# Splitting posts, operand scaling and root computations into stages, one per step, in a one-core hybrid mLSTM / short-convolution block

## The chip, the cores and the metric

The kernel runs on one core of a Trainium2 chip. The metric is the device time of one execution in microseconds (us). Engines are written as in the profile: PE is TensorE, DVE is VectorE, ACT is ScalarE, POOL is GpSimd and SP is SyncE (which here only issues loads).

## What is computed

One residual block over 512 tokens of width 2048, in float32. Cut to what matters:

```
hn   = rmsnorm(x, norm_mix_g)
proj = hn @ w_in + b_in           # q, k, v, o, i, f, cb, cc, ch, gm, gc
hm   = mlstm(q, k, v, i, f)       # 4 heads, causal, per head an RMS norm at the end
y_m  = (hm * g * sigmoid(o)) @ w_branch_m
y_c  = (cb * causal_dwconv(cc * ch, conv_w)) @ w_branch_c
h    = x + (sigmoid(gm) * y_m + sigmoid(gc) * y_c) @ w_out
u    = causal_dwconv(rmsnorm(h, norm_ffn_g) @ w_up, ffn_conv_w, ffn_conv_b)
h    = h + (silu(gate) * val) @ w_down        # gate, val = halves of u
out  = rmsnorm(h, norm_out_g)
```

## The kernel before

**Steps and items.** All large products run through one hand-written loop of 492 steps, `for s in range(4, len(steps))` (L1203). An *item* is a pair of output blocks of 128 columns: 40 items of the x projection (numbers 0 to 39: q and k, v, o, cb, the conv pairs cc and ch as 16 to 23, then the gates gm and gc), 8 each for y_c, y_m and out, 43 for up, and three chunks of 8 for down; 16 short pieces end the program. A *step* is a quarter of an item (half of one for y_c and y_m) and holds 42 matmuls of 256 columns (48 in the last quarter of some), written by `cell_mm`. Float32 products are made of three passes over a high and a low half (`wh` with `xh`, `wh` with `xl`, `wl` with `xh`: L271 to L273), and a Strassen-like scheme makes 7 products of 8 out of sums of weight blocks.

**What the engines do in a step.** ACT copies the rounded high half of the next but one step's weights (`wh`, L225), DVE forms the low half (`wl`, L229) of the next step's, and sums of weight blocks (L210, L215). `wl` has three buffers and `wh` four. When an item ends, ACT evacuates one bank (L295) and DVE the others (L301 to L304, `evac_ops`) in the step that follows. Operand cells (activations) are prepared two steps ahead by `cell_task`: DVE's t3, e, t4 (L333, L338, L343), ACT's `hi` (L347), DVE's `lo` (L350). For the up items the cells come from h, scaled by the norm's gain: by ACT inside t3 (L331; L380 and L381 where the cell comes straight out of an item's buffer, `direct_cell`), followed at once by DVE's L333.

**Posts.** After its evacuation each item has a post: a list of pieces with costs. For q, k, v, gates and cb one piece multiplies by the row of 1/rms (`normed`, L642) and adds the bias or sigmoid on ACT, then stores. Conv items have four pieces (norm and bias; product and first tap; two taps; product with cb, store). Up items have four (norm and two biases; two taps and silu; two taps; product and store). Out items have two: residual, store of h and square on ACT (L764); then the sums of squares into mC (L769, L770), and after the last of them the norm's stages. Pieces are taken in order from one queue while a credit of DVE time lasts; an item about to lose its buffer forces what is left (`flush`), at the item end (L1275 on). Stores are issued by ACT in the step after.

**Side stages.** A queue `side` gives PE one extra piece per step, behind the step's matmuls, and its post runs in the next step, behind DVE's work for the weights. All of it shares one PSUM bank, SIDE (bank 7). The four heads of the mLSTM run there: load; `b_pe` / `b_post` four times (scores, exponentials on ACT, mask on POOL, product on DVE L577); `v_pe` / `v_post` twice (transposes); `c_pe` / `c_post` four times (values; then the head's norm, one root per block, L606 to L613); `t_pe` / `t_post` twice. Between two stages that fill SIDE lies an empty one (`gap`). The root (`rsqrt_cols`, L399) is a multiply-add on DVE (L403 or L405), a square root on ACT (L406), and a reciprocal with one Newton step on DVE (L407 to L411). `rows_stages` (L423) uses it for the norms over all tokens: root, four diagonal blocks on DVE (L428), a matmul into SIDE (L431), a copy into `rstd`.

The blocks c0 to c3 and t0 of head 0 are written at steps 52, 54, 56, 58 and 60, those of the later heads 24 steps later each. Every second of them (c2, t0) falls in a step that also evacuates an item.

Of the kernel before, what the change touches and what calls it, by code (L numbers as in the profile page):

```python
# [59 lines left out]
class Task:  # L60


    def __init__(self, load, sums, hi, lo, ready=None):
        self.load, self.sums, self.hi, self.lo, self.ready = load, sums, hi, lo, ready
        self.wh = self.wl = None
        self.raw, self.cost, self.plain, self.after_end = None, (0.8, 2.05), False, None
# [3 lines left out]
def tile_block(ctx: ExitStack, tc: tile.TileContext, xT, w1, w_v0, w_v1, w_v2, w_bm, w_bc, w_out, w_up, w_down,  # L70
# [236 lines left out]
    def cell_task(xs, c, d, scale=None, key=None, eight=False):  # L307

        k1, k2 = kpair(c) if isinstance(c, int) else c
        t = Task(None, None, None, None)  # L310

        def new_raw():
            t.raw = wp.tile([P, NW], F32, tag="raw", name=nm("xraw"), bufs=RAW)

        def load():
            new_raw()
            for dst, k in zip(t.two(), (k1, k2)):
                SP.dma_start(dst, d[k])

        def two_k():  # L320
            return (t.raw[:, :T], t.raw[:, T:2 * T]) if eight else (t.raw[:, 5 * SW:], t.raw[:, :2 * SW])

        def diff():
            x = slots(t.raw)
            V.tensor_sub(x[:, 4:6], x[:, 0:4:2], x[:, 1:4:2])

        def t3():
            x = slots(t.raw)
            if scale:
                for ap, k in zip(two_k(), (k1, k2)):  # L330
                    A.activation(ap, ap, AF.Copy, scale=scale(k))  # L331

            V.tensor_sub(x[:, 2:4], x[:, 1:6:4], two(x[:, 6]))  # L333
# [24 lines left out]
        t.ready = (lambda: all(k in stored for k in key)) if key else None  # L358
        return t

    def direct_cell(xs, c, it, d=None, scale=None, key=None, eight=False):

        t = cell_task(xs, c, d, None, key, eight)
        cell_t3, cell_load = t.sums[0], t.load
        k1, k2 = kpair(c)

        def load():
            if d is not None:
                cell_load()
            else:  # L370
                t.new_raw()

        def t3():
            assert it.done
            a, b = t.two()
            if d is not None:
                V.tensor_add(a, a, it.z[:, :T])
                V.scalar_tensor_tensor(b, it.z[:, T:], -1.0, b, op0=ALU.mult, op1=ALU.subtract)
            else:
                A.activation(a, it.z[:, :T], AF.Copy, scale=scale(k1))  # L380
                A.activation(b, it.z[:, T:], AF.Copy, scale=scale(k2))  # L381
            it.z_read = True
            cell_t3()

        it.z_read = False
        t.load, t.sums = load, [t3] + t.sums[1:]
        t.cost = (t.cost[0] + (1.35 if d is not None else 0), t.cost[1])
        t.after_end = it
        return t
# [9 lines left out]
    def rsqrt_cols(dst, src, scale, eps, n):  # L399

        v, y, t = sm("nv")[:, :n], sm("ny")[:, :n], sm("nt")[:, :n]
# [4 lines left out]
        A.activation(y, v, AF.Sqrt)  # L406
        V.reciprocal(y, y)  # L407
# [15 lines left out]
    def rows_stages(ps, dst, diag, nt=4):  # L423

        def cols_post():
            rsqrt_cols(rs1[:, :nt], ps[:, :nt], 1.0 / D, EPS, nt)
# [9 lines left out]
        return cols_post, rows_pe, rows_post  # L436
# [114 lines left out]
    def head_stages(h):  # L551
# [16 lines left out]
        def b_post(cs):  # L568
            def fn():
                w = T - cs * P  # L570
                p = S[:, So[cs]:So[cs] + w]
                for ct in range(cs, 4):
# [3 lines left out]
                                fill=0.0, base=0, channel_multiplier=-1)  # L576
                V.scalar_tensor_tensor(p, SIDE[:, :w], QK_SCALE, p, op0=ALU.mult, op1=ALU.mult)  # L577
# [25 lines left out]
        def c_post(ct):  # L603
            def fn():
# [7 lines left out]
                rsqrt_cols(ff[:, c], ssq[:, c], 1.0 / DV, den[:, c], 1)  # L612
# [34 lines left out]
    def qk_post(h):  # L647
        def post(it):
            a, b = halves(it)

            def fn():
                normed(it)
# [3 lines left out]
            return [(1.2, fn)]  # L656
        return post

    def v_post(h):
        def post(it):  # L660
            a, b = halves(it)

            def fn():
                normed(it)
# [3 lines left out]
            return [(1.2, fn)]  # L668
        return post

    def sig_post(d, c, j1, j2, key):
        def post(it):
            a, b = halves(it)

            def fn():
                normed(it)
# [3 lines left out]
            return [(1.2, fn)]  # L680
        return post

    def conv_post(j):
        def post(it):
            a, b = halves(it)

            def one():
                normed(it)
# [10 lines left out]
            def four():  # L699
                V.tensor_mul(a, a, mC)  # L700
                store(yc_d[j], a, ("yc", j))
            return [(1.2, one), (0.7, two_), (1.4, three), (0.7, four)]
# [16 lines left out]
    def cb_post(p):  # L719
        def post(it):  # L720
# [3 lines left out]
            def fn():  # L724
                normed(it)
# [3 lines left out]
            return [(1.2, fn)]  # L729
# [25 lines left out]
    acc = mC  # L755

    def out_post(p):
        def post(it):
            j1, j2 = kpair(p)

            def one():
                residual(it)
                store(pair_ap(h_d, j1, j2), sb_pair(it.z), ("h", p))
                A.activation(it.buf[:, :2 * T], it.z, AF.Square)  # L764
                it.done = True

            def two_():
# [5 lines left out]
                if p == 7:  # L773
                    cols, rows_pe, rows_post = rows_stages(SIDE, rstd, mC)
                    side.append((lambda: sum_tokens(SIDE, acc, 1, 4, True, True), cols))
                    side.append((noop, noop))
                    side.append((rows_pe, rows_post))
            return [(1.3, one), (1.4, two_)]
        return post

    def up_post(j):
        def post(it):
# [3 lines left out]

            def one():
                normed(it)
# [3 lines left out]
            def two_():  # L792
                V.scalar_tensor_tensor(y0[:, 1:], a[:, :T - 1], fwc(1, j), y0[:, 1:], op0=ALU.mult, op1=ALU.add)
                V.scalar_tensor_tensor(y0[:, 2:], a[:, :T - 2], fwc(0, j), y0[:, 2:], op0=ALU.mult, op1=ALU.add)
                A.activation(y0, y0, AF.Silu)
# [4 lines left out]

            def four():
# [256 lines left out]
    def flush(upto):  # L1058

        if posts and posts[0][2] <= upto:  # L1060
            while posts and posts[0][2] <= upto:
                posts.popleft()[1]()
            flush_late()
# [122 lines left out]
    cols, rows_pe, rows_post = rows_stages(SIDE, rstd, gb[5])  # L1186
    cols()
# [15 lines left out]
    for s in range(4, len(steps)):  # L1203
# [13 lines left out]
        for i in ended:  # L1217
            credit -= 2.3
            evs += evac_ops(i)
            for cost, fn in i.post(i):  # L1220
                posts.append((cost, fn, i.num))
# [14 lines left out]
        for t in cells_at.get(s + 2, []):  # L1236
            credit -= t.cost[0]
            load_to(t)
            sms += t.sums
# [49 lines left out]
        if s >= 4 + hold:  # L1289
            credit = min(credit, 2.5)  # L1290
            while posts and (credit > posts[0][0] / 2 or any(x[2] in urgent for x in posts) or not main):
                cost, fn, _ = posts.popleft()
                credit -= cost
                fn()
        if not main and it.n == 11:
            plain_rows = bank[3]
            cols, _, _ = rows_stages(LCOLS[0], None, mC, 2)
            cols()
# [16 lines left out]
    cols, _, _ = rows_stages(LCOLS[1], None, mC, 2)  # L1315
    cols()
# [62 lines left out]
```

## Time and profile before

| | us |
|---|---|
| median of 3 runs (2686.54 to 2688.54) | 2686.89 |
| the profiled execution's own time | 2686.18 |
| its span, first to last instruction | 2684.5 |
| PE busy | 2587.5 |
| DVE busy | 2112.7 |
| ACT busy | 1278.2 |
| granted PE clock, mean | 0.990 |

The span lies inside the execution's time; the rest is start and end. A line of the waits view reads: engine, tile and line that waited, what it waited for, us in total, times, longest. A line of the time line reads: start in us from the span's start, duration, engine, line, operation, output<-inputs, and in brackets the idle time of that engine just before and what ended it. A line of windows reads: the stretch, its length, then for PE, weight loads, DVE, ACT and POOL the busy time and count, then the granted PE clock (1.00 is full), the DMA engines' share and GB/s.

### The profile page before, as it was taken

To read this page: it belongs to the slowest core of one execution; us is meant where nothing else is said; L and a number is where in the kernel's file an instruction comes from. 1 tells how busy PE (TensorE), PEld (TensorE's weight loads), DVE (VectorE), ACT (ScalarE), POOL (GpSimd) and SP (SyncE) were. 2 spreads that over 40 slices of the span, in tenths; PEclk is the share of its full clock that TensorE was granted. 3 is DMA by queue.
4 is the path that set the end of the run, shared out by engine and by line. 5 is a ranking of instruction groups with operands and counts; after the bars stand their busy time and mean duration, and the time that the engine had idled before them with its cause. 6 is when DMAs were issued, how large, how long until landed. Compare 5 with 4: busy or idle time off the path is not lost.

```text
span 2684.5 us, 55468 instructions
## 1 busy us (share of the span) xinstructions
PE 2587.5 (96%) x21148; PEld 2564.8 (96%) x21148; DVE 2112.7 (79%) x3304; ACT 1278.2 (48%) x1735; POOL 801.6 (30%) x931
## 2 busy tenths in 40 slices
PE   7899999999999999999799999999999999999998
PEld 6899998999999999899799999999999989999997
DVE  5677777887777788977889988888888887676756
ACT  6444554445554443444545444444444554444433
POOL 3343333233333211121233333333333223232320
PEclk9899999999999999999999999999999999999999
DMA  7799989898989797797788888889888889798976
GB/s 193 177 230 235 246 228 229 215 243 223 253 228 233 205 297 221 212 252 207 204 223 219 223 222 225 221 222 228 218 222 227 206 216 226 188 226 207 238 173 200
DMA packets 464860, 594.64 MB, mean 222 GB/s; under 512 B 43040, under 2 KB 299040, under 8 KB 464592
## 3 DMA queue, kind: packets, MB, share of 16 engines
q1 hardware_dynamic: 303120, 420.84, 49.5%
q0 software_dynamic: 134240, 125.09, 31.6%
q10 hardware_dynamic: 27232, 45.17, 4.6%
q8 instruction: 165, 2.70, 0.4%
q14 instruction: 103, 0.84, 0.1%
HBM read 533.26 MB, written 57.67 MB: 220 GB/s over the span
## 4 chain that ended last, share of the span: by engine, by line
PE 52%; DVE 6%; DMA 4%; issue 2%; ACT 1%; POOL 0%; SPq 0%; DVEq 0%; POOLq 0%; ACTq 0%
PE bank L273 17%; PE bank L271 17%; PE bank L272 17%; DMA raw<-in_w_down_dram 2%; DVE wl L229 2%; DVE act L350 1%; DMA raw<-in_w_out_dram 1%; DMA raw<-in_w_up_dram 1%; DVE z L302 1%; DVE z L301 0%; PE bank L420 0%; PE bank L1095 0%; PE bank L1096 0%; DVE raw L210 0%; PE bank L1097 0%
## 5 line engine op out<-in xcount | busy, mean ns | idle before, releaser
L273 PE MATMUL bank<-act,wl 128*128 128x256 f32 x6760 | 1924.0, 285 | 39.3 <-DVE wl L229 35.9
L271 PE MATMUL bank<-act,wh 128*128 128x256 f32 x6760 | 1930.9, 286 | 14.7 <-DVE z L301 8.1
L272 PE MATMUL bank<-act,wh 128*128 128x256 f32 x6760 | 1919.7, 284 | 0.3 <-DVE act L350 0.3
L273 PEld LDWEIGHTS bank<-act,wl 128*128 128x128 f32 x6760 | 1304.2, 193 | 47.2 <-DVE wl L229 42.9
L271 PEld LDWEIGHTS bank<-act,wh 128*128 128x128 f32 x6760 | 1304.4, 193 | 19.3 <-DVE z L301 9.1
L272 PEld LDWEIGHTS bank<-act,wh 128*128 128x128 f32 x6760 | 1304.2, 193 | 3.6 <-issue 1.8
L225 ACT ACTIVATE wh<-raw 128x896 fp32r<-128x896 f32 x856 | 804.0, 951 | 1018.5 <-PE bank L272 682.0
L229 DVE TENSOR_TENSOR wl<-raw,wh 128x896 fp32r<-128x896 f32 x856 | 928.5, 1086 | 220.2 <-PE bank L273 149.6
L245 POOL DMA_DIRECT2D raw<-in_w_up_dram x344 | 299.1, 957 | 616.6 <-DMA raw<-in_w_up_dram 252.1
L245 POOL DMA_DIRECT2D raw<-in_w_dram x288 | 251.2, 950 | 551.2 <-DMA raw<-in_w_dram 274.3
L210 DVE TENSOR_TENSOR raw<-raw 128x256 f32<-128x256 f32 x428 | 179.2, 419 | 40.6 <-DMA raw<-in_w_down_dram 21.6
L245 POOL DMA_DIRECT2D raw<-in_w_down_dram x112 | 100.4, 1017 | 279.8 <-DMA raw<-in_w_down_dram 126.4
L215 DVE TENSOR_TENSOR raw<-raw 128x256 f32<-128x256 f32 x428 | 178.5, 417 | 0.2
L347 ACT ACTIVATE act<-xraw 128x1792 fp32r<-128x1792 f32 (+1 forms) x52 | 85.6, 1646 | 67.3 <-DVE xraw L343 56.6
L301 DVE TENSOR_TENSOR z<-bank,z 128x512 f32<-128x512 f32 x131 | 89.9, 686 | 28.4 <-ACT z L295 17.2
L183 ACT ACTIVATE wh<-raw 128x256 fp32r<-128x256 f32 x96 | 40.0, 416 | 130.1 <-PE bank L272 117.7
L350 DVE TENSOR_TENSOR act<-xraw,act 128x1792 fp32r<-128x1792 f32 (+1 forms) x52 | 101.7, 1956 | 0.0
L642 DVE TENSOR_TENSOR z<-z,rstd 128x1024 f32<-128x1024 f32 x83 | 101.0, 1218 | 0.0
L302 DVE TENSOR_TENSOR z<-bank,z 128x512 f32<-128x512 f32 x131 | 89.6, 684 | 1.8
L304 DVE TENSOR_TENSOR z<-bank,z 128x512 f32<-128x512 f32 x131 | 89.5, 683 | 0.0
L188 DVE TENSOR_TENSOR wl<-raw,wh 128x256 fp32r<-128x256 f32 x96 | 40.4, 421 | 57.9 <-PE bank L273 33.0
L245 POOL DMA_DIRECT2D raw<-in_w_out_dram x48 | 41.8, 972 | 129.6 <-DMA raw<-in_w_out_dram 64.0
(214 smaller groups left out, 1368.5 us busy)
## 6 DMA issues: line engine op xcount, KB each, us to landing
raw<-in_w_up_dram SPq DMA_DIRECT2D x172, 512.0 KB, 5.8
raw<-in_w_dram SPq DMA_DIRECT2D x144, 512.0 KB, 5.8
raw<-in_w_up_dram SPq DMA_DIRECT2D x344, 128.0 KB, 4.2
raw<-in_w_up_dram POOLq DMA_DIRECT2D x344, 128.0 KB, 5.1
raw<-in_w_down_dram SPq DMA_DIRECT2D x80, 512.0 KB, 5.2
raw<-in_w_dram SPq DMA_DIRECT2D x288, 128.0 KB, 4.1
raw<-in_w_dram POOLq DMA_DIRECT2D x288, 128.0 KB, 5.2
raw<-in_w_out_dram SPq DMA_DIRECT2D x32, 512.0 KB, 5.2
```

The source lines that it names most:

```text
L210: V.tensor_add(x[:, 6], x[:, 5], x[:, 0])
L215: V.tensor_add(x[:, 2], x[:, 6], x[:, 1])
L225: A.activation(seven(t.wh[r]), half(r), AF.Copy)
L229: V.tensor_sub(seven(t.wl[r]), half(r), seven(f(t.wh[r])))
L245: G.dma_start(at(i), a21, accum_op=ALU.add)
L271: PE.matmul(ps, h, xh, start=start, stop=False, skip_group_check=True)
L272: PE.matmul(ps, h, xl, start=False, stop=False, skip_group_check=True)
L273: PE.matmul(ps, l, xh, start=False, stop=stop, skip_group_check=True)
L301: return [lambda: V.tensor_add(z[:, 0:4:3], b0, two(z[:, 1])), lambda: V.tensor_add(z[:, 1:3], b1, two(z[:, 3])), lambda: V.tensor_add(z[: ...
L302: lambda: V.tensor_add(z[:, 1:3], b1, two(z[:, 3])),
L350: V.tensor_sub(t.act[:, NW:NW + m], t.raw[:, :m], f(t.act[:, :m]))
L642: V.tensor_mul(sb_pair(it.z), sb_pair(it.z), two(rstd))
```

## The change

The same instructions are issued with the same operands; their order and the step in which they stand change.

- *Posts.* The first piece of every post is now the norm on DVE alone; bias, sigmoid and store come as the next piece. Conv items: norm; bias; product and first tap; two taps, product with cb and store together. Up items: norm; biases; first two taps; silu and the other two taps; product and store. Out items: residual and store; square; sums. The queue holds items, not pieces: in a step at most one piece each of the first two items is taken. `flush` takes all that is left of an item at once.
- *Scaling.* ACT's scaling of a cell (`scaled`) is taken out of t3 and issued at the end of the step before, if the cell is loaded and the item is done; otherwise where it stood, before t3.
- *Roots.* `rsqrt_cols` becomes `rsqrt_a` (multiply-add and square root) and `rsqrt_b` (the rest). `c_post` keeps the first, and `c_post2` with `rsqrt_b` and ACT's last scaling (which reads SIDE) takes the place of the gap; `b_post2` with DVE's product (which reads SIDE) does so behind `b_post`. The norm before the up items gets one stage more, and an up item's norm asserts that it was issued.

The core of the diff:

```diff
@@ cell_task
+        def scaled():
+            for ap, k in zip(two_k(), (k1, k2)):
+                A.activation(ap, ap, AF.Copy, scale=scale(k))
         def t3():
             x = slots(t.raw)
-            if scale:
-                for ap, k in zip(two_k(), (k1, k2)):
-                    A.activation(ap, ap, AF.Copy, scale=scale(k))
...
+        t.pre = scaled if scale else None
@@ rsqrt
-    def rsqrt_cols(dst, src, scale, eps, n):
+    def rsqrt_a(src, scale, eps, n):
...
         A.activation(y, v, AF.Sqrt)
+
+    def rsqrt_b(dst, n):
+        v, y, t = sm("nv")[:, :n], sm("ny")[:, :n], sm("nt")[:, :n]
         V.reciprocal(y, y)
@@ heads
+        def b_post2(cs):
+            def fn():
+                w = T - cs * P
+                p = S[:, So[cs]:So[cs] + w]
                 V.scalar_tensor_tensor(p, SIDE[:, :w], QK_SCALE, p, op0=ALU.mult, op1=ALU.mult)
...
-                rsqrt_cols(ff[:, c], ssq[:, c], 1.0 / DV, den[:, c], 1)
+                rsqrt_a(ssq[:, c], 1.0 / DV, den[:, c], 1)
+            return fn
+
+        def c_post2(ct):
+            def fn():
+                c = slice(ct, ct + 1)
+                hn = z2[:, ct * DV:(ct + 1) * DV]
+                rsqrt_b(ff[:, c], 1)
                 A.activation(hn, SIDE[:, :DV], AF.Copy, scale=ff[:, c])
...
-            out += [(b_pe(cs), b_post(cs)), gap]
+            out += [(b_pe(cs), b_post(cs)), (noop, b_post2(cs))]
...
-            out += [(c_pe(ct), c_post(ct)), gap]
+            out += [(c_pe(ct), c_post(ct)), (noop, c_post2(ct))]
@@ posts (q and k; v, gates and cb alike)
             def fn():
-                normed(it)
                 A.activation(a, a, AF.Identity, bias=bias(C_Q + h))
...
-            return [(1.2, fn)]
+            return [(1.2, lambda: normed(it)), (0, fn)]
@@ conv_post
-            return [(1.2, one), (0.7, two_), (1.4, three), (0.7, four)]
+            return [(1.2, lambda: normed(it)), (0, one), (0.7, two_), (2.1, three)]
@@ out_post
             def one():
                 residual(it)
                 store(pair_ap(h_d, j1, j2), sb_pair(it.z), ("h", p))
+                it.done = True
+            def square():
                 A.activation(it.buf[:, :2 * T], it.z, AF.Square)
-                it.done = True
...
-                    side.append((lambda: sum_tokens(SIDE, acc, 1, 4, True, True), cols))
+                    side.append((lambda: sum_tokens(SIDE, acc, 1, 4, True, True), cols_a))
+                    side.append((noop, cols_b))
                     side.append((noop, noop))
-                    side.append((rows_pe, rows_post))
-            return [(1.3, one), (1.4, two_)]
+                    side.append((rows_pe, rows_post_up))
+            return [(1.3, one), (0, square), (1.4, two_)]
@@ up_post
-            return [(1.2, one), (1.4, two_), (1.4, three), (0.7, four)]
+            return [(1.2, norm), (0, one), (1.4, two_), (1.4, lambda: (silu(), three())), (0.7, four)]
@@ main loop
-            while posts and (credit > posts[0][0] / 2 or any(x[2] in urgent for x in posts) or not main):
-                cost, fn, _ = posts.popleft()
+            rush = not main or any(x[0] in urgent for x in posts)
+            for x in list(posts)[:2]:
+                cost, fn = x[1][0]
+                if not rush and cost and credit <= cost / 2:
+                    break
+                x[1].popleft()
                 credit -= cost
                 fn()
+                if not x[1]:
+                    posts.remove(x)
+        for t in cells_at.get(s + 3, []):
+            if t.pre and t.raw is not None and (not t.after_end or t.after_end.done):
+                t.pre()
+                t.pre = None
```

How the instructions move, on DVE. First, steps 55 and 56, in head 0 (den, nv, ny, nt and ff belong to the head's root; raw and wl to the weights; z and bank to the evacuation of an item). Before:

```order
L609 TENSOR_TENSOR den<-den,ecol 128x1
L610 TENSOR_TENSOR den<-den 128x1
L611 TENSOR_SCALAR den<-den 128x1
L405 SCALAR_TENSOR_TENSOR nv<-ssq,den 128x1
L407 RECIPROCAL ny<-ny 128x1
L408 TENSOR_TENSOR nt<-ny 128x1
L409 TENSOR_TENSOR nt<-nt,nv 128x1
L410 TENSOR_SCALAR nt<-nt 128x1
L411 TENSOR_TENSOR ff<-ny,nt 128x1
L210 TENSOR_TENSOR raw_3731<-raw_3731 128x256
```

After, the same place up to the second part of the root:

```order
L413 SCALAR_TENSOR_TENSOR nv<-ssq,den 128x1
L210 TENSOR_TENSOR raw_3731<-raw_3731 128x256
L301 TENSOR_TENSOR z_93<-bank_84,z_93 128x2x256
L215 TENSOR_TENSOR raw_3731<-raw_3731 128x256
L302 TENSOR_TENSOR z_93<-bank_85,z_93 128x512
L303 TENSOR_TENSOR z_93<-bank_85,z_93 128x256
L229 TENSOR_TENSOR wl_4008<-raw_3670,wh_3939 128x896
L304 TENSOR_TENSOR z_93<-bank_86,z_93 128x512
L229 TENSOR_TENSOR wl_4011<-raw_3670,wh_3993 128x896
L419 RECIPROCAL ny<-ny 128x1
L420 TENSOR_TENSOR nt<-ny 128x1
L421 TENSOR_TENSOR nt<-nt,nv 128x1
```

Reciprocal and Newton step moved from ahead of the next step's weights and evacuation to behind them.

Second, the change from out to up items, from the residual of the last but one out item (buffer mA) on; mC holds the sums of squares. Before:

```order
L752 TENSOR_TENSOR z_92<-mA,z_92 128x512
L753 TENSOR_TENSOR z_92<-mA,z_92 128x512
L769 TENSOR_TENSOR mC<-mC,mA 128x512
L770 TENSOR_TENSOR mC<-mC,mA 128x512
L210 TENSOR_TENSOR raw_14813<-raw_14813 128x256
```

After, where the residual is followed at once by the next step's L210 and the sums stand two steps further on:

```order
L351 TENSOR_TENSOR act_14956<-xraw_14742,act_14956 128x1792
L339 SCALAR_TENSOR_TENSOR xraw_14819<-xraw_14819 128x256
L344 SCALAR_TENSOR_TENSOR xraw_14819<-xraw_14819 128x256
L793 TENSOR_TENSOR mC<-mC,mA 128x512
L794 TENSOR_TENSOR mC<-mC,mA 128x512
L210 TENSOR_TENSOR raw_14963<-raw_14963 128x256
```

The sums moved from right behind the residual to two steps later, behind the cell work (act, xraw).

More of the change, by code (lines that the diff above doesn't have):

```diff
@@ L65, in __init__ @@
         self.wh = self.wl = None
-        self.raw, self.cost, self.plain, self.after_end = None, (0.8, 2.05), False, None
+        self.raw, self.cost, self.plain, self.after_end, self.pre = None, (0.8, 2.05), False, None, None
 @with_exitstack
@@ L375, in t3, with scaled @@
             a, b = t.two()
[L376 to L381, printed above, removed]
+            V.tensor_add(a, a, it.z[:, :T])
+            V.scalar_tensor_tensor(b, it.z[:, T:], -1.0, b, op0=ALU.mult, op1=ALU.subtract)
             it.z_read = True
             cell_t3()
-        it.z_read = False
-        t.load, t.sums = load, [t3] + t.sums[1:]
+        def scaled():
+            assert it.done
+            for ap, z, k in zip(t.two(), (it.z[:, :T], it.z[:, T:]), (k1, k2)):
+                A.activation(ap, z, AF.Copy, scale=scale(k))
+            it.z_read = True
+        it.z_read = False
+        t.load = load
+        if d is not None:
+            t.sums = [t3] + t.sums[1:]
+        else:
+            t.pre = scaled
         t.cost = (t.cost[0] + (1.35 if d is not None else 0), t.cost[1])
@@ L423, in rows_stages, with cols_a, cols_b @@
     def rows_stages(ps, dst, diag, nt=4):
-        def cols_post():
-            rsqrt_cols(rs1[:, :nt], ps[:, :nt], 1.0 / D, EPS, nt)
+        def cols_a():
+            rsqrt_a(ps[:, :nt], 1.0 / D, EPS, nt)
+        def cols_b():
+            rsqrt_b(rs1[:, :nt], nt)
             for t in range(nt):
@@ L773, in two_, with rows_post_up @@
                 if p == 7:
-                    cols, rows_pe, rows_post = rows_stages(SIDE, rstd, mC)
-                    side.append((lambda: sum_tokens(SIDE, acc, 1, 4, True, True), cols))
+                    cols_a, cols_b, rows_pe, rows_post = rows_stages(SIDE, rstd, mC)
+                    def rows_post_up():
+                        rows_post()
+                        normal["up"] = True
+                    side.append((lambda: sum_tokens(SIDE, acc, 1, 4, True, True), cols_a))
+                    side.append((noop, cols_b))
                     side.append((noop, noop))
-                    side.append((rows_pe, rows_post))
-            return [(1.3, one), (1.4, two_)]
+                    side.append((rows_pe, rows_post_up))
+            return [(1.3, one), (0, square), (1.4, two_)]
         return post
@@ L785, in post, with norm @@
             y0, y1 = buf[:, :T], buf[:, T:2 * T]
+            def norm():
+                assert normal["up"]
+                normed(it)
             def one():
-                normed(it)
                 A.activation(y0, a, AF.Identity, scale=fwc(2, j), bias=fwc(3, j))
@@ L799, in three, with silu @@
                 V.scalar_tensor_tensor(y1[:, 2:], b[:, :T - 2], fw_neg(0, j), y1[:, 2:], op0=ALU.mult, op1=ALU.add)
+            def silu():
+                A.activation(y0, y0, AF.Silu)
             def four():
@@ L1058, in flush @@
     def flush(upto):
-        if posts and posts[0][2] <= upto:
-            while posts and posts[0][2] <= upto:
-                posts.popleft()[1]()
+        if posts and posts[0][0] <= upto:
+            while posts and posts[0][0] <= upto:
+                for _, fn in posts.popleft()[1]:
+                    fn()
             flush_late()
@@ L1185, in tile_block @@
     A.activation(gb[4], GATE, AF.Copy, scale=mrow)
-    cols, rows_pe, rows_post = rows_stages(SIDE, rstd, gb[5])
-    cols()
+    cols_a, cols_b, rows_pe, rows_post = rows_stages(SIDE, rstd, gb[5])
+    cols_a()
+    cols_b()
     def rows_post2():
@@ L1219, in tile_block @@
             evs += evac_ops(i)
-            for cost, fn in i.post(i):
-                posts.append((cost, fn, i.num))
+            posts.append((i.num, deque(i.post(i))))
         ended = []
@@ L1314, in tile_block @@
         last_scale(0, finals.popleft(), row0)
-    cols, _, _ = rows_stages(LCOLS[1], None, mC, 2)
-    cols()
+    cols_a, cols_b, _, _ = rows_stages(LCOLS[1], None, mC, 2)
+    cols_a()
+    cols_b()
     PE.matmul(SIDE[:, :H2], ones, mC[:, :H2], start=True, stop=True)
```

26 lines of the change are left out of this document (12 added, 14 removed).

## The prediction

> **What bounds the kernel now.** I read the page's first part, then the waits of PE, then the windows and time lines of the places where PE waits.
>
> ```profile
> span 2684.5 us, 55468 instructions
> PE 2587.5 (96%) x21148; PEld 2564.8 (96%) x21148; DVE 2112.7 (79%) x3304; ACT 1278.2 (48%) x1735; POOL 801.6 (30%) x931
> ```
>
> PE is busy 96% of the span; no other engine comes near. So only PE's waits can change the time. The waits view, PE alone:
>
> ```profile
> PE bank L273 <- DVE wl L229: 35.9, 29, 3.7
> PE bank L271 <- DVE z L301: 8.1, 5, 3.2
> PE bank L584 <- ACT mB L593: 3.4, 2, 1.7
> PE bank L431 <- DVE mC L428: 3.3, 1, 3.3
> PE bank L621 <- DVE mB L627: 2.3, 4, 1.8
> ```
>
> PE waits for DVE's low halves of the weights (wl), for evacuations (z), and for stages on the shared SIDE bank. It is late only where DVE falls behind. Three places hold what the change touches: steps 223 to 229, where the out items hand over to the up items; some early up items; and the four mLSTM heads.
>
> The matmuls' own time, step 55 to 56 (head 0):
>
> ```profile
> 360.04 0.28 PE L273 MATMUL bank<-act,wl 128*128 128x256 f32 x1
> 360.16 0.28 PE L271 MATMUL bank<-act,wh 128*128 128x256 f32 x1
> 365.20 1.47 PE L600 MATMUL bank<-mB,mA 128*128 128x258 f32 x6
> ```
>
> Matmuls start 0.12 us apart but show 0.28, so a stall costs its idle time plus 0.16. Step 56 has 42 of them, from 360.16 to 365.20, and then c_pe, the head's matmul into SIDE. In the kernel before it starts at once.
>
> **Gain 1: steps 223 to 229.** DVE's and PE's waits between 1270 and 1335, then the rows of the second RMS norm's chain:
>
> ```profile
> DVE xraw L333 <- ACT xraw L381: 3.9, 3, 1.3
> DVE mC L769 <- ACT mB L764: 1.6, 1, 1.6
> DVE mC L769 <- ACT mA L764: 1.2, 1, 1.2
> ...
> 1318.80 0.15 DVE L403 TENSOR_SCALAR nv<-bank 128x4 f32<-128x4 f32 x1
> 1321.06 0.42 DVE L210 TENSOR_TENSOR raw<-raw 128x256 f32<-128x256 f32 x1
> ```
>
> DVE is the limit here: PE waits for its L301 and L229. The square gets a step of its own, so the sums L769 no longer wait (1.6 + 1.2 = 2.8). ACT scales the direct cells at the end of the step before, so L333 doesn't wait (3.9). The chain from L403 to L210 (2.26) moves one and two steps on, where DVE has caught up. Sum 9.0 us of DVE, and PE follows DVE: -9.0. What is late next: still L301 and L229, about 2 us a step until DVE has caught up, so nothing beyond this is won. Bounds: -4, if ACT (hi, then square, then scaling) is itself late and half of 9.0 returns; -10 with the chain's own PE wait (3.3) not fully counted.
>
> **Gain 2: up items**, PE's waits between 1385 and 1480:
>
> ```profile
> PE bank L273 <- DVE wl L229: 3.4, 4, 1.3
> ...
> DVE mB L793 <- ACT mB L789: 35.9, 19, 2.5
> DVE mA L793 <- ACT mA L789: 33.7, 19, 1.9
> ```
>
> (The last two are of the whole span.) The taps L793 wait 1.8 us each for the bias of the same step; a step apart they won't. Four PE stalls go: 3.4 + 4 x 0.16 = -4.0. The other 34 waits of DVE are covered by its slack already: nothing. Bounds -2 and -4.4.
>
> **Gain 3: heads.** PE's waits between 430 and 620:
>
> ```profile
> PE bank L273 <- DVE wl L229: 3.9, 3, 1.7
> PE bank L584 <- ACT mB L593: 3.4, 2, 1.7
> PE bank L621 <- DVE mB L627: 1.8, 1, 1.8
> ```
>
> They stem from conv posts bunched with head stages; spread over steps they go: 9.1, and 0.5 of L621 in the other heads, with 9 x 0.16: -11.0. Bounds -7 and -11.
>
> **Cost 1: the split root.** c_post2 runs in the very step at whose end PE overwrites SIDE (c_pe of the next block, or t_pe), and its last instruction reads SIDE. In the order before a whole step lay between. So PE waits where the end of c_post2 is later than the step's last matmul. Rows of head 0, DVE and ACT, and one table load of head 2:
>
> ```profile
> 357.91 1.09 DVE L229 TENSOR_TENSOR wl<-raw,wh 128x896 fp32r<-128x896 f32 x1 [1.97 <-PE bank L273]
> 358.92 0.15 DVE L609 TENSOR_TENSOR den<-den,ecol 128x1 f32<-128x1 f32 x1
> 359.56 0.16 DVE L405 SCALAR_TENSOR_TENSOR nv<-ssq,den 128x1 f32<-128x1 f32 x1
> 359.99 0.16 DVE L407 RECIPROCAL ny<-ny 128x1 f32<-128x1 f32 x1 [0.27 <-ACT ny L406]
> 361.79 0.69 DVE L301 TENSOR_TENSOR z<-bank,z 128x512 f32<-128x512 f32 x1 [0.53 <-ACT z L295]
> 366.39 1.22 DVE L642 TENSOR_TENSOR z<-z,rstd 128x1024 f32<-128x1024 f32 x1
> ...
> 358.89 0.20 ACT L608 ACTIVATION_READ_ACCUMULATOR z<-bank 128x1 f32 x1
> 359.75 0.20 ACT L406 ACTIVATE ny<-nv 128x1 f32<-128x1 f32 x1 [0.66 <-DVE nv L405]
> 361.01 0.47 ACT L613 ACTIVATE z<-bank,ff 128x256 f32<-128x256 f32 x1 [1.06 <-DVE ff L411]
> 361.39 0.38 ACT L295 ACTIVATE z<-bank 128x256 f32<-128x256 f32 x1
> ...
> 642.26 1.28 ACT L406 ACT_TABLE_LOAD   x1
> ```
>
> From L407 to the end of L613 is 359.99 to 361.48: 1.49 us. Each head waits four times.
> - Plain steps (c1, c3): wl is done at 358.92, 1.24 ahead of the matmuls' end (360.16), since wl has three buffers and must wait for PE. 1.49 - 1.24 and some 0.1 for signals: 0.4 each, 8 times, 3.2.
> - Steps that also evacuate an item (c2, t0), head 0: L405 ends 359.72, the root 359.95, L295 360.33, L301 starts 360.36; the evacuation and both wl take 361.79 to 366.39, 4.60: 364.96; plus 1.49: 366.45, against 365.20: 1.3 each, 2.6.
> - The same in heads 2 and 3: sigmoid posts lie between, so a table load (1.28) stands between L608's end (359.09) and the root, and once an ACT store (0.37): L301 at 361.0 to 361.4, and 1.9 to 2.3, say 2.1, four times: 8.4.
> - Head 1: the conv taps and the product now run as one stage in the step ahead of the evacuation:
>
> ```profile
> L697 DVE SCALAR_TENSOR_TENSOR z<-z,pneg 128x510 f32<-128x510 f32 x8 | 6.0, 750 | 0.3
> L696 DVE SCALAR_TENSOR_TENSOR z<-z,pneg 128x511 f32<-128x511 f32 x8 | 6.0, 744 | 0.0
> L700 DVE TENSOR_TENSOR z<-z,mC 128x512 f32<-128x512 f32 x8 | 5.5, 693 | 0.3
> ```
>
> Together 2.19: after 359.72 they put L210 (0.34) at 361.91, the evacuation's end at 366.85, L613's at 368.34, against 365.20: 3.2 each, two times, 6.4. By the same addition b_post2, moved a step on, makes v_pe or b_pe late three times in heads 1 and 2 (0.8, 0.8, 0.4): 2.0.
>
> Sum 3.2 + 2.6 + 8.4 + 6.4 + 2.0 = +22.6. No row of before shows c_pe waiting so; the nearest is L621 <- L627, a stage of the same step (2.3 in four waits). Bounds: 16 waits at the plain 0.4 give 6.4; 28 if stores and table loads all come late. I take the sum, since each term is an addition of rows. Behind the waiting PE stands all of the next step.
>
> **Cost 2: the clock.** Three stretches with stalls:
>
> ```profile
> 459.90:469.52 9.62, 6.19 (x51) 5.78 (x50) 9.24 (x14) 4.75 (x8) 3.11 (x5) 1.00 0.78 187
> 1294.45:1305.07 10.62, 8.58 (x50) 8.12 (x51) 8.91 (x15) 5.67 (x6) 1.75 (x2) 0.68 0.57 153
> 2227.50:2237.60 10.10, 7.06 (x44) 6.65 (x44) 9.44 (x14) 2.42 (x4) 2.60 (x3) 0.83 0.73 161
> ...
> 2233.18 0.38 PE L271 MATMUL bank<-act,wh 128*128 128x256 f32 x1 [2.45 <-ACT z L295]
> ```
>
> The first holds two stalls of 1.7 and keeps full clock; the third holds one of 2.45 and has 0.83; the second, behind one of 3.2, has 0.68. So between 1.7 and 2.45 us of waiting PE's clock begins to fall; 0.83 of 10.10 is 1.7 us lost. Head 1's two waits of 3.2 would cost 1.7 each: +3.4. Bounds 0 and +10 (the four waits of 2.1 too). The Trainium skill ("TensorE: Matmul & The Clock Gate", Part 1: The HAM clock gate) says that the clock halves after at least one idle window of about 3.4 us, which is free-running: by it 3.2 us would cost nothing and the sum would be 3.4 lower. The trace's 2.45 speaks against that.
>
> In steps 223 to 229 the same fall costs nothing of its own, as DVE is the limit there.
>
> **Cost 3: the change to the down items.** At the end of steps 403 and 407 the posts of the items before must be done at once (flush), and the evacuation L295 queues on ACT behind their store:
>
> ```profile
> 2232.37 0.33 ACTq L147 DMA_DIRECT2D a_d<-mB  x1
> ```
>
> PE waits for that L295 until 2233.18 (above). With one stage per step, norm (1.22, row 366.39) and two taps that had run a step earlier now stand in front of that store as well: about 2.7 us more DVE work in that step, less 1.4 that it no longer carries over: 1.3 later. In 407 the same list meets a step that had slack: 1.3 again. +2.6; bounds 0 and +5.
>
> **Covered.** ACT gets three table loads more (3 x 1.28): ACT is busy 48%, and only the two on the root's way are counted (above). SP's load of sigmoid(o) into mB comes one step later, still a step ahead of its reader. Nothing else is added or removed: the same instructions in another order.
>
> **Sum**, on the profiled execution's own 2686.18 us (span 2684.5 and 1.7 around it): -9.0 - 4.0 - 11.0 + 22.6 + 3.4 + 2.6 = +4.6, 2690.8. That execution is 0.7 below the median of the runs, 2686.89, so against it 2691.5: 0.17% slower. What a measurement here can tell from no change is about 0.2%, 5.4 us.
>
> **Rivals.**
> - *The clock doesn't fall* (chance 0.15): both 3.2-us waits end before the clock reacts, and PE goes on at full rate. For it: the two stalls of 1.7 with clock 1.00; against: 2.45 with 0.83. Sum +1.2: 2688.1. The rule of the Trainium skill quoted above would have it so.
> - *Slower* (0.22): the waits of 2.1 us in heads 2 and 3 fall on the clock's side too. One mechanism: a wait over about 2 us in c2 or t0 halves the clock, 4 x 1.7 = +6.8: 2698.3. It decides from the point where L301 starts over 0.8 us into the step. For it: 2.1 is nearer to 2.45 than to 1.7; against: the two stalls of 1.7 in one stretch kept theirs.
> - *Faster* (0.13): the 16 waits are all near the plain 0.4, because without L613 ahead of L295 the evacuation starts early enough and DVE catches up. Then 6.4 + 2.0 and no clock loss: -9.0 - 4.0 - 11.0 + 8.4 + 2.6 = -13.0: 2673.9. Against it: 4.60 us of evacuation and wl follow L301 back to back in the rows, whatever comes before.
> - *Nothing is moved* (0.05): the freed waits were hidden by other waits that come next, and c_post2 is hidden too: 2686.9. Against it: PE's waits in the three places name just these instructions.
>
> **Chances.** My forecast, +4.6 and some 4 us to either side, has 0.45: two thirds of it (0.30) within 5.4 us, the rest (0.15) slower. With the clock rival (0.15) and nothing moved (0.05) within, that is same 0.50; slower 0.15 + 0.22 = 0.37; faster 0.13. The range takes in the slower rival and 4 us of its unknown costs, and downward the removal of gains at full with waits half as long: 2681 to 2702; what is left out is most of the faster rival and costs at their upper ends together.
>
> **What would show it.** In the changed kernel's profile: DVE no longer waits for ACT at the sums and at L334 (L333 before), nor at the up taps; PE reaches step 230 about 9 us sooner after step 223 begins; between 1385 and 1480 PE has no stall. In the heads PE's waits name ACT's scaling L641 (L613 before), 16 times, some 20 us, longest 3.2, and PEclk falls near steps 80 and 84. Wrong would be: c_pe waiting under 8 us in total (then it is faster), PE stalls left in steps 224 to 229 of the old size, or a new wait in a phase that I left out, yc to out.

## The result, and the profile after

The changed kernel took 2694.4 us (median of 14 runs, 2687.54 to 2698.05), the kernel before 2686.31 (14 runs beside it, 2680.35 to 2692.99): ratio 1.0031, 95% interval 1.0022 to 1.0041. It is slower, by 8 us. Runs of one kernel scatter by some 5 us to either side, so single terms below come from the traces, and the times carry the sums.

Top of the page and PE's waits in the kernel after, to be laid beside those of before. A line number of after is up to some 35 higher: L580 is b_pe, L621 c_pe, L649 t_pe, L641 the last scaling of the head (L613 before).

```profile
span 2692.6 us, 55546 instructions
PE 2589.0 (96%) x21148; PEld 2565.4 (95%) x21148; DVE 2111.6 (78%) x3304; ACT 1284.0 (48%) x1738; POOL 805.4 (30%) x931
```

```profile
PE bank L273 <- DVE wl L229: 27.0, 19, 3.7
PE bank L271 <- ACT z L295: 11.0, 4, 5.6
PE bank L621 <- ACT z L641: 8.0, 8, 2.9
PE bank L649 <- ACT z L641: 7.4, 4, 2.9
PE bank L580 <- DMA mB<-qk_d: 5.3, 2, 3.3
PE bank L271 <- DVE z L301: 4.5, 3, 3.3
```

The busy times are nearly those of before. The waits for DVE's weights and evacuations fell (35.9 to 27.0, 8.1 to 4.5), the wait for the norm's matmul is gone, and so are those for L593 and L627. New are 15.4 us for the head's last scaling; the wait for the load of q and k rose from 0.9 to 5.3, and that for the first evacuation, L295, from 6.7 to 11.0. The windows between the same steps say where the time went; first the kernel before: steps 41 to 136 (heads), 223 to 230, 230 to 404, 404 to 409.

```profile
280.30:804.93 524.63, 514.13 (x4168) 506.37 (x4167) 397.26 (x698) 275.30 (x419) 170.21 (x210) 1.00 0.90 233
1277.05:1334.82 57.77, 43.64 (x312) 41.26 (x311) 48.12 (x75) 30.63 (x36) 13.96 (x16) 0.91 0.73 191
1334.82:2227.56 892.74, 882.94 (x7323) 880.51 (x7321) 787.92 (x1148) 435.12 (x532) 300.11 (x346) 1.00 0.88 223
2227.56:2258.53 30.97, 27.93 (x219) 27.52 (x218) 26.20 (x40) 12.78 (x20) 9.41 (x10) 0.94 0.75 170
```

And after, between the same steps:

```profile
280.82:825.68 544.86, 523.63 (x4169) 513.72 (x4167) 400.00 (x698) 279.53 (x422) 174.38 (x209) 0.98 0.88 224
1297.81:1346.28 48.47, 41.62 (x310) 40.25 (x309) 45.86 (x66) 29.05 (x34) 13.80 (x16) 0.93 0.82 214
1346.28:2232.51 886.23, 880.70 (x7324) 879.08 (x7323) 784.00 (x1155) 436.34 (x530) 298.89 (x345) 1.00 0.89 225
2232.51:2266.60 34.09, 27.81 (x218) 27.40 (x217) 26.08 (x40) 14.84 (x22) 11.28 (x12) 0.90 0.78 178
```

The heads lost 20.2 us, and the clock there is 0.98 instead of 1.00. The change from out to up won 9.3, the up items and what follows 6.5; the first down items lost 3.1. Sum: +7.5, of the span's 8.1.

Why the heads lost: step 80 (c2 of head 1) in the kernel after, DVE, then ACT, then PE. Its matmuls began at 497.52 and ended at 502.56.

```profile
496.93 0.16 DVE L413 SCALAR_TENSOR_TENSOR nv<-ssq,den 128x1 f32<-128x1 f32 x1
497.01 0.75 DVE L720 SCALAR_TENSOR_TENSOR z<-z,pneg 128x511 f32<-128x511 f32 x1
499.52 0.68 DVE L301 TENSOR_TENSOR z<-bank,z 128x512 f32<-128x512 f32 x1
504.11 0.16 DVE L419 RECIPROCAL ny<-ny 128x1 f32<-128x1 f32 x1
...
505.13 0.47 ACT L641 ACTIVATE z<-bank,ff 128x256 f32<-128x256 f32 x1 [3.49 <-DVE ff L423]
...
505.66 2.40 PE L621 MATMUL bank<-mB,mA 128*128 128x258 f32 x6 [2.94 <-ACT z L641]
```

Taps and product (497.01 to 499.18) stand ahead of the evacuation, the evacuation and the weights (4.59 from L301 on) ahead of the root's second part, and ACT's scaling is done 3.1 us after PE could have begun c_pe. This is the chain of the prediction.

And the clock, behind that wait (steps 80 and 81), behind the load at step 89, and behind a wait of 1.7 us (step 104):

```profile
497.50:507.40 9.90, 6.96 (x49) 6.45 (x48) 9.66 (x19) 3.32 (x5) 1.72 (x2) 0.94 0.71 182
507.40:513.70 6.30, 6.30 (x45) 6.18 (x44) 2.45 (x8) 1.58 (x5) 1.75 (x2) 0.82 0.70 148
555.90:565.20 9.30, 6.04 (x49) 5.83 (x48) 7.00 (x10) 3.47 (x4) 1.75 (x2) 0.95 0.96 257
565.20:572.90 7.70, 7.70 (x44) 7.70 (x44) 2.09 (x3) 2.64 (x3) 3.62 (x5) 0.62 0.82 222
643.40:651.50 8.10, 6.40 (x51) 6.06 (x49) 7.20 (x15) 3.79 (x7) 1.72 (x2) 1.00 0.89 248
```

The first pair lost 9.90 x 0.06 + 6.30 x 0.18 = 1.7 us of clock, the second 0.5 + 2.9 = 3.4, the last nothing. The load at step 65, for which PE waits 2.0 us, is followed by a fall too: half the clock for 3.45 us, 1.7 us lost.

```profile
420.90:424.35 3.45, 3.45 (x18) 3.45 (x18) 0.00 (x0) 0.00 (x0) 1.35 (x2) 0.51 0.67 251
```

### The profile page after: what moved, and what is told of

Read it like the earlier page. It is cut to its first block, busy times and chain, and to the rows that moved or that the text cites. A ratio compares the mean times of both kernels' runs of the same rounds, so it can differ in the third digit from the quotient of the medians.

```text
span 2692.6 us, 55546 instructions
## 1 busy us (share of the span) xinstructions
PE 2589.0 (96%) x21148; PEld 2565.4 (95%) x21148; DVE 2111.6 (78%) x3304; ACT 1284.0 (48%) x1738; POOL 805.4 (30%) x931
## 4 chain that ended last, share of the span: by engine, by line
PE 81%; DVE 8%; DMA 4%; issue 2%; ACT 1%; POOL 0%; SPq 0%; DVEq 0%; ACTq 0%; POOLq 0%
PE bank L273 26%; PE bank L271 26%; PE bank L272 26%; DVE wl L229 2%; DMA raw<-in_w_down_dram 2%; PE bank L621 1%; DVE act L351 1%; DMA mB<-qk_d 1%; DVE z L302 1%; PE bank L432 0%; DVE z L304 0%; PE bank L1131 0%; DVE z L301 0%; DMA raw<-in_w_up_dram 0%; PE bank L1132 0%
## 5 line engine op out<-in xcount | busy, mean ns | idle before, releaser
L225 ACT ACTIVATE wh<-raw 128x896 fp32r<-128x896 f32 x856 | 813.1, 953 | 1083.7 <-PE bank L272 726.3
L210 DVE TENSOR_TENSOR raw<-raw 128x256 f32<-128x256 f32 x428 | 180.0, 421 | 42.1 <-DMA raw<-in_w_down_dram 23.6
L301 DVE TENSOR_TENSOR z<-bank,z 128x512 f32<-128x512 f32 x131 | 89.8, 685 | 27.7 <-ACT z L295 17.6
```

The lines of the kernel that those rows point to most:

```text
L210: V.tensor_add(x[:, 6], x[:, 5], x[:, 0])
L225: A.activation(seven(t.wh[r]), half(r), AF.Copy)
L301: return [lambda: V.tensor_add(z[:, 0:4:3], b0, two(z[:, 1])), lambda: V.tensor_add(z[:, 1:3], b1, two(z[:, 3])), lambda: V.tensor_add(z[: ...
```

## The experiments

All of them compute the whole block. The ratios are to the kernel before, which ran beside each; the changed kernel's is 1.0031.

**c_whole: the head's root in one piece again**

```diff
-            out += [(c_pe(ct), c_post(ct)), (noop, c_post2(ct))]
+            out += [(c_pe(ct), lambda a=c_post(ct), b=c_post2(ct): (a(), b())), gap]
```

> The changed kernel with the head's root in one piece again: c_post does what c_post and c_post2 do, and an empty stage follows, as before the change; all other splits stay. Theory (PE waits because c_post2 reads SIDE in the step at whose end PE overwrites it): the 12 waits for L641 (15.4 us idle, some 17 with 0.16 each) and the clock that falls behind the two of 2.9 us (about 2.5) go, little comes back: about 19 us less than the changed kernel, 2675, ratio to the kernel before 0.996. Rival 1 (the root's DVE work costs the same wherever it stands, PE then waits for wl instead): ratio stays at 1.003. Rival 2 (the late loads of q and k into mB, 5.3 us of PE waits in the changed kernel, also come from c_post2, which issues a load one step later): 8 us more go, ratio 0.993.

Measured: 2676.56 us, ratio 0.9959 (0.9947 to 0.9971). PE's waits in its heads (300 to 830):

```profile
PE bank L580 <- DMA mB<-qk_d: 4.2, 2, 2.9
PE bank L649 <- DVE mB L655: 2.4, 4, 1.0
PE bank L273 <- DVE wl L229: 0.4, 1, 0.4
```

All waits for L641 are gone and wl takes their place with 0.4 only, so rival 1 falls. (The 2.4 us at L655 stood in the kernel before too, 2.3 at L627.) The loads of q and k are still waited for, so rival 2 falls too. One line of the change turns the gain of the rest into a loss.

**root_only: the kernel before with the split root alone**

```diff
-                rsqrt_cols(ff[:, c], ssq[:, c], 1.0 / DV, den[:, c], 1)
+                rsqrt_a(ssq[:, c], 1.0 / DV, den[:, c], 1)
+            return fn
+
+        def c_post2(ct):
...
-            out += [(c_pe(ct), c_post(ct)), gap]
+            out += [(c_pe(ct), c_post(ct)), (noop, c_post2(ct))]
```

> The kernel before with one part of the change alone: c_post split into c_post and c_post2. Theory: 16 waits at c1, c2, c3 and t0, 0.4 in plain steps and 1.3 to 3.2 where an item is evacuated, and some clock: +15 to +24 us, ratio 1.006 to 1.009. Rival (the wait is hidden where posts run as before the change, or the other splits cause it): within 3 us, ratio 1.000.

Measured: 2698.46 us, ratio 1.0042 (1.003 to 1.0054), so about +11 by the ratio. PE's waits in its heads; its lines L608, L636 and L628 are c_pe, t_pe and the scaling:

```profile
PE bank L608 <- ACT z L628: 6.8, 7, 1.8
PE bank L636 <- ACT z L628: 4.5, 4, 1.3
PE bank L592 <- ACT mB L601: 2.2, 2, 1.5
PE bank L273 <- DVE wl L229: 2.1, 1, 2.1
PE bank L573 <- DMA mB<-qk_d: 0.7, 2, 0.4
```

The split alone slows the kernel, and the rival falls; but less than expected. By the lengths of the sixteen steps that end with such a wait (from a step's first main matmul to the next step's) the split costs 16.0 us here, inside the expectation. But old stalls shrink beside it (steps 74, 85 and 98 by 2.2, 1.9 and 2.3), which the expectation left out. Where posts run as before, no taps stand ahead of the evacuation and no table load ahead of the root there, so c2 and t0 cost PE 1.3 to 1.5 in every head. The clock stays at 1.00 in these heads, behind the 2.1 us for wl (step 70) too:

```profile
441.10:454.30 13.20, 11.12 (x89) 10.53 (x87) 11.26 (x17) 6.48 (x10) 2.40 (x4) 1.00 0.82 186
```

The long waits of the changed kernel are the split root and the split posts together. The load is waited for 0.7 only, and step 89 is as short as in the kernel before (5.2 us): the late load at head 2 comes with the posts.

**c_copy: c_post2 doesn't read SIDE**

```diff
+                A.activation(hn, SIDE[:, :DV], AF.Copy)     # at the end of c_post
-                A.activation(hn, SIDE[:, :DV], AF.Copy, scale=ff[:, c])
+                A.activation(hn, hn, AF.Copy, scale=ff[:, c])
```

> The changed kernel, but c_post copies SIDE to z2 unscaled (one ACT instruction of about 0.47 us more per block), and c_post2 scales z2 in place, so c_post2 no longer reads SIDE. It computes the same. Theory (it is the read of SIDE that PE waits for): the waits of c1 to c3 go (0.4, 1.3 to 3.2 and 0.4 per head, 8.0 us idle by the profile of the changed kernel, some 9 with 0.16 each, and about 1 to 1.5 of clock), those of t0 stay (7.4 idle), since it reads what c_post2 writes: about 10 to 13 us less than the changed kernel, ratio 0.998 to 0.9995. Rival (PE waits because DVE is late with the root, whichever bank is read; wl would be late next): no gain, ratio 1.003.

Measured: 2679.31 us, ratio 0.9974 (0.9961 to 0.9988). PE's waits in the heads:

```profile
PE bank L650 <- ACT z L642: 7.0, 4, 2.6
PE bank L580 <- DMA mB<-qk_d: 4.4, 3, 2.9
```

All eight c_pe waits are gone and the four of t_pe stay, though DVE's root is just as late (in step 80 its second part begins 6.6 us into the step in both kernels). So at c_pe it is the read of the shared bank that held PE, as the theory says; t_pe waits for the scaled values themselves. The gain is about 15 us, 2 more than its upper end, of which the load at step 65 and the clock behind it are some 3 (a wait that scatters, see below).

**conv_early: a shorter conv piece ahead of the evacuation**

```diff
-            return [(1.2, lambda: normed(it)), (0, one), (0.7, two_), (2.1, three)]
+            return [(1.2, lambda: (normed(it), one())), (0.7, two_), (1.4, three), (0.7, four)]
```

> The changed kernel with the conv posts in another division: norm and bias in one step, product and first tap in the next, two taps in the third, and in the last step of the item only the product with cb (0.69 us on DVE) instead of taps and product (2.19). Theory (the waits of head 1 at c2 and t0 are long because 2.19 us stand ahead of the evacuation, and a wait of 2.9 us lets the clock fall where one of 1.7 does not): these two waits shrink by about 1.5 each, and two clock falls (about 1.2 each) go: 5 to 5.5 us less than the changed kernel, ratio 1.001. Rival 1 (the clock falls all the same): 3 us less, ratio 1.002. Rival 2 (the length of the conv piece does not matter): ratio 1.003.

Measured: 2684.27 us, ratio 0.9994 (0.9985 to 1.0002). Waits in the heads, and steps 80 and 81:

```profile
PE bank L621 <- ACT z L641: 6.0, 5, 1.7
PE bank L649 <- ACT z L641: 5.8, 4, 1.7
PE bank L580 <- DMA mB<-qk_d: 3.2, 1, 3.2
```

```profile
493.50:501.20 7.70, 6.34 (x49) 6.02 (x48) 7.53 (x17) 3.65 (x6) 1.72 (x2) 1.00 0.81 219
501.20:506.50 5.30, 5.30 (x45) 5.25 (x45) 3.12 (x8) 1.81 (x6) 1.75 (x2) 1.00 0.87 188
```

No wait for L641 is longer than 1.7, and the clock stays at 1.00 behind them: both as expected, so both rivals fall. (The profile is of an execution 5 us above the median.) The time fell by 10 instead of 5. In the two profiles the load at head 1, not waited for here (2.0 in the changed kernel), makes up 3.6 of the heads' 10.6. But up to that load both kernels run the same instructions in the same order, so that wait comes and goes between executions, and why the medians differ by 5 us more than expected stays open.

**no_pre: c_whole without the early scaling**

```diff
-            if t.pre and t.raw is not None and (not t.after_end or t.after_end.done):
+            if False:
```

> The changed kernel with the head's root in one piece (c_whole), and besides with ACT's scaling of the up items' cells back in the step of the subtraction that needs it. Theory (in steps 223 to 229 DVE is the limit and waits for this scaling): DVE's waits for ACT at L334 return, 3.9 us as in the kernel before, and PE gets to step 230 about 3 to 4 us later than in c_whole: 2680, ratio 0.9973. Rival (the gain in these steps comes from the sums and the root alone, the scaling is hidden since the square no longer stands ahead of it on ACT): no difference from c_whole, ratio 0.996.

Measured: 2681.72 us, ratio 0.9976 (0.9965 to 0.9987): about 4.5 more than c_whole, with intervals that just overlap. DVE's waits between 1255 and 1330:

```profile
DVE xraw L334 <- ACT xraw L325: 4.1, 4, 1.6
DVE xraw L334 <- ACT xraw L386: 3.9, 3, 1.3
```

The 3.9 are back to the digit, and so are the waits for L325, the scaling of cells that were loaded from memory (L331 in the kernel before: 5.1 between the same times). Steps 223 to 229, in c_whole and then here:

```profile
1278.87:1326.73 47.86, 41.34 (x311) 40.18 (x310) 45.37 (x66) 28.80 (x33) 13.12 (x16) 0.93 0.81 214
1278.22:1332.84 54.62, 44.16 (x310) 42.83 (x309) 48.71 (x73) 31.91 (x36) 14.81 (x17) 0.88 0.80 212
```

The scaling is worth 6.8 us in these steps, more than the 3 to 4 expected, and also where the square no longer stands ahead of it; the rival falls. (The other kernels that scale early take 47.1 to 48.7 here.)

**qk_first: the load of q and k ahead of the gates**

```diff
+            SP.dma_start(qk[:, :2 * T], qk_d[h])
             SP.dma_start(S[:, :T], gates_d[32 * h:32 * h + 1, :].to_broadcast([P, T]))
-            SP.dma_start(qk[:, :2 * T], qk_d[h])
```

> c_whole with the head's load of q and k into mB issued ahead of the broadcast load of the gates instead of behind it. Theory (PE waits at b3 of heads 1 and 2 because this load takes 10 us, in the queue behind 256 KB of the gates and beside the weights): the load lands 1 to 2 us sooner, the two waits of 4.2 us in total become 1 to 2, and the clock falls behind neither: 3 to 5 us less than c_whole, ratio 0.9945. Rival (the load waits for the store of the head before out of mB, not for the queue, or all queues share what the engines move): no difference, ratio 0.996.

Measured: 2672.32 us, ratio 0.9943 (0.993 to 0.9955), 4 less than c_whole, with overlapping intervals. One wait for the load is left, at head 2:

```profile
PE bank L580 <- DMA mB<-qk_d: 1.6, 1, 1.6
```

**tail: the last up posts without waiting for credit**

```diff
-            rush = not main or any(x[0] in urgent for x in posts)
+            rush = not main or any(x[0] in urgent for x in posts) or 401 <= s <= 407
```

> c_whole with the posts of the last two up items taken one piece per step in steps 401 to 407 whether there is credit or not, so that the forced flush at the end of steps 403 and 407 finds less. Theory (PE waits in 404 and 408 for L295, which ACT runs behind the store that ends the flushed post): norm and bias of both items move ahead, the wait in 404 (4.8 us in c_whole) shrinks by 2 to 3, the one in 408 goes: 2.5 to 4 us less than c_whole, ratio 0.9945 to 0.995. Rival (DVE is late with wl there as soon as it gets work earlier, as it is limiting in 395 to 400): 0 to 2 us slower than c_whole, ratio 0.996 to 0.997.

Measured: 2675.2 us, ratio 0.9951 (0.9938 to 0.9963). PE's wait there between 2200 and 2260, in c_whole:

```profile
PE bank L271 <- ACT z L295: 5.5, 2, 4.8
```

and in tail:

```profile
PE bank L271 <- ACT z L295: 3.9, 1, 3.9
```

The wait in 408 goes and that in 404 shrinks by 0.9, less than the 2 to 3 expected (in both, with the same edit, it is 2.1 in all). The median is 1.4 below c_whole's, and the two intervals overlap: the trace shows the mechanism, the time alone wouldn't.

**late_cb: cb's load behind the weights on SP.** In the changed kernel SP's queue waits between 440 and 580 show a new first line, which the kernel before doesn't have:

```profile
SPq L731 <- DVE raw L210: 43.0, 6, 9.0
```

L731 loads cb for the next conv item into mC. It must wait for the product of the item before, which now comes last in the step. (The view names L210, which DVE runs right behind the product; at head 2 the product ends at 552.40 and L731 goes at 552.43.) SP works in order, so weights, gates, q and k queue behind it and start together, between 552.9 and 554.9.

```diff
-            SP.dma_start(mC, cb_d[j])
+            behind.append(lambda: SP.dma_start(mC, cb_d[j]))      # issued after loads()
```

> c_whole with the load of cb into mC (needed by a conv item's product) issued by SP behind the weight loads of its step instead of ahead of them. Theory (in the changed kernel this load waits 6 to 8 us for the product of the conv item before, which the change put at the end of that step, and holds up the weight and head loads queued behind it on SP, so that the load of q and k lands late at head 2): SP's wait at L731 goes or holds up nothing, the wait for q and k at step 89 (2.9 us in c_whole) goes and the clock there stays: 3 to 6 us less than c_whole, ratio 0.994 to 0.9948. The wait at step 65 stays, as no conv item has ended by then. Rival (it is the gates' broadcast and the engines' share alone, as in qk_first): no difference, ratio 0.996.

Measured: 2672.82 us, ratio 0.9951 (0.9937 to 0.9966). PE's wait for the load, both heads:

```profile
PE bank L580 <- DMA mB<-qk_d: 1.2, 2, 0.8
```

4.2 became 1.2, and nothing of it is over 0.8, so the clock stays; the median is 3.7 below c_whole's, with overlapping intervals. The profile is of the fastest of the six executions, but step 89 alone says the same: 6.3 us, against 8.6, 9.0 and 9.0 in c_whole, no_pre and tail, whose order there differs in this load alone. The queue was one cause of the late load at head 2: q and k now start 2.6 us ahead of step 89 instead of 1.4, and land after 8.6 us instead of 9.4. The other is their place behind the gates (in qk_first they land after 7.8). The wait at step 65, expected to stay, went from 1.3 to 0.4; but it is 0 in no_pre and 0.5 in tail, so this is not late_cb's doing.

**both: qk_first and tail together**

> c_whole with qk_first and tail together, as a version that may beat the other ones. If each is worth what its theory says, 5 to 9 us less than c_whole: 2669, ratio 0.993 to 0.994. If neither: ratio 0.996.

Measured: 2666.97 us, ratio 0.9922 (0.9908 to 0.9935): some 20 us less than the kernel before and the lowest median here.

**all3: with late_cb as well**

> c_whole with qk_first, tail and late_cb together. If late_cb takes away what qk_first left at step 89 (1.6 us and 0.16), 2 us less than both: 2665, ratio 0.9915. If they are worth the same thing twice, as both: 0.992.

Measured: 2667.44 us, ratio 0.9931 (0.9916 to 0.9945), no better than both. What late_cb could still add there, 2 us, is too little for these intervals.

## Why the prediction was right or wrong

The measured ratio, 1.0031, lies inside the range, and the main mechanism, gains at DVE's waits outweighed by PE's waits for c_post2, is what the traces and c_whole show. But the likeliest case, +4.6 and most of it "no change", was too low: 8 us is past the 5.4 that I took for the border. By the terms (the steps' lengths in the two traces compared):

| term | predicted | measured |
|---|---|---|
| steps 223 to 229 | -9.0 | -9.3, and +0.9 in the two steps behind |
| up items | -4.0 | -4.4 |
| head stalls removed | -11.0 | -11.7 |
| waits for c_post2, with clock | +20.6 and 3.4 | +22.8 |
| b_post2 late at v_pe or b_pe | +2.0 | +0.4 |
| first down items | +2.6 | +3.1 |
| loads of q and k | 0 | +8.9, clock included |
| change from up to down | 0 | -3.0 |

- *Gain 1* was right in its sum and not in its parts. Between 1290 and 1350 DVE's waits in the kernel after no longer name ACT; the first is now a load:

```profile
DVE raw L210 <- DMA raw<-in_w_up_dram: 3.1, 2, 2.1
DVE wl L188 <- PE bank L273: 1.8, 1, 1.8
```

  The +0.9 is the norm's own matmul into SIDE, which moved with its stage from step 227 to the end of step 230. With it, 8.4 is won:

```profile
1351.33 1.02 PE L446 MATMUL bank<-mC,ones 128*128 128x512 f32 x2
```

  The prediction priced the scaling at 3.9, from the cells that come straight out of an item's buffer. Its view of DVE's waits (1270 to 1335, kernel before) has one more line, for cells loaded from memory, which the sum put at nothing:

```profile
DVE xraw L333 <- ACT xraw L331: 3.1, 2, 1.9
```

  By no_pre the scaling is worth 6.8; without it the steps win 57.8 - 54.6 - 0.9 = 2.3, and that is all the sums and the root have together, where 2.8 and 2.3 were forecast. That the parts add up to the forecast is in part luck. The sums and the root weren't tried apart.
- *Gain 2* was right; between 1385 and 1480 the kernel after has no PE wait at all.
- *Gain 3* was right in size. Of its reason one piece fails: the waits at L627 (2.3) didn't go with the spread posts, since c_whole has these and keeps 2.4 at the same instruction (L655). They go only where the root is split.
- *Cost 1* was right step by step: 0.4 in plain steps, 1.3 for c2 and t0 of head 0 (1.0 of it idle in the view), 1.9 in heads 2 and 3 (2.1 predicted), 3.1 in head 1 (3.2). All sixteen steps are longer, as forecast, though the view of waits names only twelve, with 15.4 us idle. c_copy shows that at c_pe the read of SIDE is what counts. The long waits need the new place of the posts too: in root_only the sixteen steps cost 16.0, and none loses clock. The rival "faster", all waits at 0.4, fails as I argued: 4.6 us stand behind L301.
- *Cost 1's last part*, b_post2 late by 0.8, 0.8 and 0.4, failed in size: steps 73, 93 and 97 are longer by 0.2 each and one other is shorter. Why DVE is less late there than I added up wasn't looked into.
- *Cost 2* was right in its sum: two waits of 2.9 idle lost some 1.7 us of clock each, and the four of 1.7 in heads 2 and 3 kept it, so the slower rival fell. The price came from the row behind 2.45 us; the prediction's own row behind 3.2 us (0.68 of 10.62) gives 3.4, which is what the 3.3 us at step 89 did cost. Nor does the length of a wait alone decide: 2.0 us at step 65 lost 1.7, and 2.1 us in root_only lost nothing. The rule of the Trainium skill ("TensorE: Matmul & The Clock Gate", Part 1: The HAM clock gate), an idle window of about 3.4 us, doesn't fit: 2.0 to 2.9 were enough here.
- *Cost 3* was right in place, and 0.5 too low; tail and both show that the flushed post is the cause.
- *Covered* is the step that failed. I looked at SP's load of sigmoid(o), which was harmless, and not at the load of cb: at head 2 it had to wait for a product that the change had moved to the end of the step, and held up SP's queue. With the gates ahead of it, the load of q and k took 9.9 and 10.3 us to land (heads 2 and 1) instead of 5.1 and 8.1, PE waited 5.3 us instead of 0.9, and twice the clock fell. These steps are 8.9 longer than in the kernel before, more than the whole gap between forecast and result. Of this, 6.3 belong to head 2 and come back in each kernel with the new posts and the unchanged order of loads: step 89 takes 8.3 to 9.0 us in six of them, and 5.2 in the kernel before and in root_only. late_cb and qk_first show two causes. The 2.6 at head 1 don't come back: conv_early issues the same instructions in the same order as the changed kernel until then, and its load lands after 7.8 us instead of 10.3 and step 65 takes 5.3 us instead of 7.4 (6.3 in the kernel before). So this part is scatter between executions, and that qk_first has no wait there proves nothing (no_pre, with the load behind the gates, has none either).
- The -3.0 at steps 394 to 400 isn't explained: there the same steps take up to 5 us more or less in other kernels with the same order (10.9 us in c_whole's step 395, 6.0 in the changed kernel's), so it is left as scatter of the loads. Without it the loss would be 11 us, still inside the range but more than twice the forecast; that the total came out so near is luck in this part.

## What to carry to other kernels

Splitting work over steps helps where an engine truly waits for another within a step, and it must be checked for what each later piece still holds: a bank that the next stage overwrites, a buffer that a load is queued for. Moving the read of a shared buffer later moves its release later; copy it out early, which helps those who wait for the buffer but not those who need the value, or leave the reader where it was, and split only the rest. A queue that works in order turns one load's wait for a late reader into late loads for everyone behind it: list what the moved instruction frees, and who waits for that on every queue, before calling a move free.

## What the runs showed that was not expected

- Idle times of 1.7 us left PE's granted clock at 1.00; 2.0, 2.45 and 2.9 us lost 1.7 us of it, and 3.3 us (step 89) lost 3.4. But 2.1 us in root_only lost nothing, so between these lengths something besides the length counts; which, no run here shows.
- The same load of 512 KB (head 2) landed after 5.1 us in one order and after 9.9 in another (9.4 to 10.7 in five more kernels with that order), with the DMA engines busy over 0.9 of the time in both.
- Where a table load stands ahead of the root, PE's step is longer by 0.4 to 0.7 us at each of four places (1.9 or 2.0 over the kernel before in the changed kernel, 1.3 to 1.5 in root_only, which has none there), though ACT is busy 48% of the span.
